# Down projection of an encoder kernel: loading rows into idle activation buffers, raising the corner splits' priority, and moving two late sums behind the first update of x

## The chip, the cores and the metric

The kernel runs on one core of one Trainium2 chip. The metric is device time in microseconds (us), the median of the runs shown; for the kernel before it is 1094.71 us.

The engines are named as the profile names them. PE is the matrix engine and PEld its weight load, DVE the vector engine, ACT the scalar engine, POOL the general engine, SP the engine that issues nearly all loads. A `q` behind a name is that engine's queue.

## The reference, cut to what matters

Two layers work on 256 tokens of 1024 numbers. Each layer is a gated feed-forward part of half weight, an attention part, and a second feed-forward part. The change touches the feed-forward part alone, and there the last product, the down projection by `w_down`:

```python
def swiglu(x, w_gate, w_up, w_down):
    return (jax.nn.silu(x @ w_gate) * (x @ w_up)) @ w_down

x = x + 0.5 * swiglu(rms_norm(x, ffn1_norm[l]), ffn1_w_gate[l], ffn1_w_up[l], ffn1_w_down[l])
```

`w_down` is 2816 x 1024, so a layer has two down projections and the program has four.

## The kernel before, in words

**Tiles.** The tokens lie in T = 2 tiles of 128 partitions. The 2816 inner columns are cut into NFC = 11 chunks of 256. For each chunk and token tile the gate and up columns are multiplied (24 matmuls of 512 columns in `project`), ACT makes the silu (`sg`), DVE the product (`hh`, line 435), and PE turns it round (`turn`). When all chunks have been started, `down` multiplies by `w_down`.

**Three products for one.** All large products are split: a value is written as a high part, rounded by ACT (line 181), and a low part, the rest, which DVE subtracts (line 182). `three` (lines 166 to 169) then issues three matmuls: high by high, low by high, high by low. The high and low parts of weights are `wh` and `wl`, in rings of 6 buffers; what comes from memory is `raw`, in a ring of RAW = 4 buffers of 512 KB. A new load into a `raw` buffer waits until the four-back user has been read by ACT and DVE.

**Seven products for eight.** A chunk c of the down projection takes two blocks of 128 rows of `w_down`, r0 = row block 2c and r1 = 2c + 1, each of two halves of 512 columns. `PLAN = "SFGFGFGSGSS"` says how each chunk is done. S is plain: 8 products of a 128 x 128 block by 512 columns (two rows, two token tiles, two halves). F and G do it with 7 products of sums and differences. Those need the corner (the first half of r0, split into `ch` and `cl`), the two halves of r1, and two tiles of differences: u holds r1 - r0 of the second halves and the difference of r0's halves, v holds r1's halves less parts of u. DVE makes u and v in four subtractions (line 343), and both are split like any weight. For F chunks (1, 3, 5) the differences are made and split earlier, during the gate and up products, and stored, so that `sevens` loads only half of r0 and all of r1 (256 and 512 KB). For G chunks (2, 4, 6, 8), the unprepared pairs, everything is done in place, and both rows are loaded whole. In all cases product "1", the corner, comes first. I write F1, G2, F3, G4, F5, G6, S7, G8, S9, S10 for the chunks by number.

**The corner has one pair of buffers.** `ch` and `cl` lie in the two buffers of tag `xg`; the next chunk's corner can be split only when PE has read the present one.

**The end.** The seven products gather in seven banks; after G8, `combine` adds the banks into x: lines 405 to 418 make the sums `p1`, `p16` and `ends` and add three of them, with the bank of product "1", to the four quarters of x. The last chunks S9 and S10 go on gathering in four banks, in `out_rows`, and for each quarter (t, d) line 299 adds half of the bank to x at high priority. Four products after a quarter's last one, `norm` starts on that quarter for the next stage: PE turns it round (line 198). In the fourth feed-forward part the quarters are stored instead.

**What orders the work.** PE's order is the order in which the code is written. On the other engines and on SP a scheduler sets it, by priorities and by its own forecast of time; each engine then works strictly in that order, so a waiting instruction holds all behind it.

**The idle buffers.** The normalized input of a feed-forward part is kept in four tiles, `xh0`, `xl0`, `xh1`, `xl1` (high and low part of the two token tiles), of 4 KB a partition each, as large as a `raw` buffer. PE reads them in `project` alone; after chunk 10's gate and up product of a token tile nothing reads that tile's pair until the next `norm` writes it.

Of the kernel before, what the change touches and what calls it, by code (L numbers as in the profile page):

```python
# [11 lines left out]
F32 = mybir.dt.float32  # L12
# [4 lines left out]
ALU = mybir.AluOpType  # L17
# [4 lines left out]
P = 128  # L22
# [4 lines left out]
T = S // P  # L27
KD = D // P
FC = 256
NFC = FF // FC  # L30
# [11 lines left out]
RAW = 4  # L42
# [13 lines left out]
def hybrid_encoder(ctx, tc, x, w_gu1, w_d1, w_in, b_gate, qk_gain, rpb, sink, t5,  # L56
# [123 lines left out]
    def split_to(hi, lo, src):  # L180
        linked("act", lambda: nc.scalar.activation(hi, src, AF.Copy))  # L181
        linked("dve", lambda: nc.vector.tensor_tensor(lo, src, hi.bitcast(F32), ALU.subtract))  # L182
# [99 lines left out]
        tag, n = ACC[t][d]  # L282
        return ps_acc.tile([P, 512], F32, name="acc", tag=tag, bufs=n)

    def out_rows(get, acc, k0, k1, last, w, l, scale, after):
        pieces = [(k, *rows(w, l, k)) for k in range(k0, k1)]
        for t in range(T):
            for d in range(2):
                for k, wh, wl in pieces:
                    first = acc[t][d] is None  # L290
                    if first:
                        acc[t][d] = out_bank(t, d)
                    xh, xl = get(t, k)
                    three(acc[t][d], xh, xl, wh[:, d, :], wl[:, d, :], first, last and k == k1 - 1)
                    tick(1)
                if last:
                    xd = xs[t][:, d * 512:(d + 1) * 512]
                    with tc.high_priority(500):
                        nc.vector.scalar_tensor_tensor(xd, acc[t][d], scale, xd, op0=ALU.mult, op1=ALU.add)
                    after(t, d)  # L300

    def ffn(l, n, w_gu, w_d, after):
        with tc.tile_pool(name="ffn", bufs=1) as fp:
# [30 lines left out]

            stored = {}

            def block_row(k, c0=0, n=2):
                r = ring.tile([P, 2, 512], F32, name="raw", tag="raw", bufs=RAW)[:, :n, :]
                nc.sync.dma_start(r, w_d[l, k * P:(k + 1) * P, :n * 512].rearrange("p (h n) -> p h n", h=n))
                return r  # L340

# [28 lines left out]

            def down():
                acc = [[None] * 2 for _ in range(T)]
                banks = {"2": (0, 0), "3": (0, 1), "4": (1, 0)}
                extra = {}
                c = 0
                while c < NFC:
                    if PLAN[c] == "S":
                        end = NFC if "S" * (NFC - c) == PLAN[c:] else c + 1
                        out_rows(get, acc, 2 * c, 2 * end, end == NFC, w_d, l, 0.5, after)
                        c = end  # L380
                        continue
                    final = c == max(PLAN.rindex("F"), PLAN.rindex("G"))
                    for name, slot, (wh, wl) in sevens(c):
                        if name in banks:
                            t, d = banks[name]
                            first = acc[t][d] is None
                            if first:
                                acc[t][d] = out_bank(t, d)
                            bank = acc[t][d]
                        else:  # L390
                            first = name not in extra
                            if first:
                                pool, tag = (ps_g, "g") if name in "16" else (ps_tp, "tp")
                                extra[name] = pool.tile([P, 512], F32, name=tag, tag=tag)
                            bank = extra[name]
                        three(bank, *[h[:, slot, :] for h in hs[c]], wh, wl, first, final and name in extra)
                        tick(1)
                    if final:
                        combine(extra)
                    c += 1  # L400

            def combine(acc):
# [4 lines left out]
                def plus(to, name, x):  # L407
                    nc.vector.scalar_tensor_tensor(to, acc[name], 0.5, x, op0=ALU.mult, op1=ALU.add)
                    return to

                u2 = plus(p1[:, 1, :], "6", p1[:, 0, :])
                u3 = plus(p16[:, 0, :], "7", u2)
                u4 = plus(p16[:, 1, :], "5", u2)
                u5 = plus(ends, "5", u3)
                plus(xs[0][:, :512], "1", xs[0][:, :512])
                for (t, d), u in (((0, 1), u4), ((1, 0), u3), ((1, 1), u5)):
                    xd = xs[t][:, d * 512:(d + 1) * 512]
                    nc.vector.tensor_tensor(xd, xd, u, ALU.add)

            for c in range(NFC):  # L420
                first = n == 0 and c == 0
# [391 lines left out]
```

## Time and profile before

| | |
|---|---|
| median of 3 runs | 1094.71 us (1093.98 to 1096.26) |
| profiled execution | 1094.91 us, of which the span is 1093.1 us |
| busy in the span: PE, PEld, DVE | 1079.0, 889.3, 855.3 us |
| busy: ACT, POOL | 659.2, 116.2 us |
| granted TensorE clock | 1.0 |
| loads | 211.60 MB through SP's queue, 61.5% of 16 engines' span |

The profile is of one execution. The page gives sums over the whole span; the timeline gives instructions in order of time with, in brackets, how long the engine was idle before and what ended it; the list of waits groups these idle times; the chain shows what was released by what, back from the last instruction. A matmul's duration overlaps the next one, so that its worth in time is the step from one start to the next. The first down projection's matmuls start at 135.4 us, and its next stage at about 194 us.

### The profile page before, as it was taken

What the parts mean: (1) busy time and instruction counts of PE and PEld (TensorE: products, weight loads), DVE (VectorE), ACT (ScalarE), POOL (GpSimd) and SP (SyncE); (2) the same over time, 40 slices, a digit from 0 to 9 for tenths busy, and PEclk for the clock granted to TensorE, in tenths of its full rate; (3) what the DMA queues carried; (4) which work ended last, traced back from release to release, by engine and by line L of the source; (5) the groups of instructions that cost most, each with busy time, mean ns of one, the idle gap of its engine ahead of it and who ended that gap; (6) DMA issues with size and microseconds to landing.
All of it is one profiled execution on the core that took longest, in us unless ns stands there. A gap on an engine that the chain in (4) does not pass through costs nothing.

```text
span 1093.1 us, 14659 instructions
## 1 busy us (share of the span) xinstructions
PE 1079.0 (99%) x5137; PEld 889.3 (81%) x5137; DVE 855.3 (78%) x1298; ACT 659.2 (60%) x1002; POOL 116.2 (11%) x118
## 2 busy tenths in 40 slices
PE   9999999999999999999999999999999999999998
PEld 7888878888888888887888888788888888888877
DVE  6887778889886778776877786787888767878676
ACT  6665544788764566554465665457877546656442
POOL 1400000243510000000000000003534000000000
PEclk9999999999999999999999999999999999999999
DMA  7876556765654666654757665557666555776553
GB/s 239 267 222 210 185 169 206 232 189 154 192 176 136 209 213 214 210 194 149 245 175 227 215 217 168 189 161 236 185 186 182 177 168 162 226 234 202 183 174 105
DMA packets 98827, 212.62 MB, mean 195 GB/s; under 512 B 7569, under 2 KB 13745, under 8 KB 98753
## 3 DMA queue, kind: packets, MB, share of 16 engines
q1 hardware_dynamic: 98560, 211.60, 61.5%
q8 instruction: 40, 0.66, 0.2%
q0 software_dynamic: 192, 0.08, 0.1%
q14 instruction: 35, 0.28, 0.1%
HBM read 210.59 MB, written 1.06 MB: 194 GB/s over the span
## 4 chain that ended last, share of the span: by engine, by line
PE 78%; DVE 10%; DMA 6%; issue 3%; ACT 3%; DVEq 0%; ACTq 0%
PE g L168 19%; PE g L169 19%; PE g L167 19%; DMA raw<-in_w_d 4%; DVE wl L182 4%; PE acc L167 4%; PE acc L168 4%; PE acc L169 4%; PE tp L314 2%; ACT wh L181 2%; PE tp L198 1%; DVE v L343 1%; PE g L234 1%; PE pt L557 1%; PE sc L536 1%
## 5 line engine op out<-in xcount | busy, mean ns | idle before, releaser
L182 DVE TENSOR_TENSOR wl<-raw,wh 128x1024 fp32r<-128x1024 f32 (+1 forms) x340 | 408.1, 1215 | 66.8 <-ACT wh L181 65.2
L181 ACT ACTIVATE wh<-raw 128x1024 fp32r<-128x1024 f32 (+1 forms) x340 | 349.8, 1045 | 158.6 <-DMA raw<-in_w_d 41.0
L167 PE MATMUL g<-wh,xh 128*128 128x512 f32 (+1 forms) x976 | 389.9, 399 | 0.0
L169 PE MATMUL g<-wh,xl 128*128 128x512 f32 (+1 forms) x976 | 379.0, 388 | 0.0
L168 PE MATMUL g<-wl,xh 128*128 128x512 f32 (+1 forms) x976 | 377.4, 387 | 0.4 <-DVE wl L182 0.4
L169 PEld LDWEIGHTS g<-wh,xl 128*128 128x128 f32 x976 | 183.3, 188 | 40.4 <-DVE xl L182 1.1
L168 PEld LDWEIGHTS g<-wl,xh 128*128 128x128 f32 x976 | 184.0, 189 | 32.1 <-DVE wl L182 0.8
L167 PEld LDWEIGHTS g<-wh,xh 128*128 128x128 f32 x976 | 183.5, 188 | 30.8 <-DVE hh L435 0.2
L433 ACT ACTIVATE sg<-g,rs_y 128x256 f32<-128x256 f32 x88 | 41.5, 471 | 135.3 <-PE g L169 133.8
L343 DVE TENSOR_TENSOR u<-raw 128x512 f32<-128x512 f32 x56 | 38.8, 693 | 79.5 <-DMA raw<-in_w_d 79.2
L167 PE MATMUL acc<-wh,hi 128*128 128x512 f32 x200 | 78.9, 395 | 0.0
L169 PE MATMUL acc<-wh,lo 128*128 128x512 f32 x200 | 78.0, 390 | 0.0
L168 PE MATMUL acc<-wl,hi 128*128 128x512 f32 x200 | 77.9, 389 | 0.0
L173 POOL TENSOR_TENSOR rs_y<-ms,mhalf 128x1 f32<-128x1 f32 x12 | 7.2, 602 | 659.5 <-DVE ms L219 652.5
L435 DVE SCALAR_TENSOR_TENSOR hh<-g,rs_y,sg 128x256 f32<-128x256 f32 x88 | 42.1, 479 | 38.2 <-ACT sg L433 38.0
L549 POOL TENSOR_TENSOR S<-S,sm 128x512 f32<-128x512 f32 x32 | 37.1, 1161 | 71.4 <-DVE sm L548 45.2
L169 PEld LDWEIGHTS acc<-wh,lo 128*128 128x128 f32 x200 | 37.5, 188 | 8.1
L168 PEld LDWEIGHTS acc<-wl,hi 128*128 128x128 f32 x200 | 37.6, 188 | 7.7
L167 PEld LDWEIGHTS acc<-wh,hi 128*128 128x128 f32 x200 | 37.6, 188 | 7.6
L542 ACT ACTIVATE S<-S,mx 128x256 f32<-128x256 f32 x64 | 31.8, 498 | 7.5 <-DVE mx L539 7.4
L314 PEld LDWEIGHTS tp<-ident,hh 128*128 128x128 f32 x176 | 24.5, 140 | 11.7 <-DVE hh L435 0.6
L314 PE MATMUL tp<-ident,hh 128*128 128x128 f32 x176 | 33.4, 272 | 0.0
(190 smaller groups left out, 1460.0 us busy)
## 6 DMA issues: line engine op xcount, KB each, us to landing
raw<-in_w_gu SPq DMA_DIRECT2D x176, 512.0 KB, 4.4
raw<-in_w_d SPq DMA_DIRECT2D x100, 512.0 KB, 4.4
raw<-in_w_in SPq DMA_DIRECT2D x64, 512.0 KB, 4.6
raw<-in_w_out SPq DMA_DIRECT2D x16, 512.0 KB, 3.5
bb<-in_b_gate SPq DMA_DIRECT2D x16, 256.0 KB, 3.7
raw<-in_w_bsw SPq DMA_DIRECT2D x8, 512.0 KB, 4.4
raw<-in_w_bna SPq DMA_DIRECT2D x8, 512.0 KB, 3.5
raw<-in_w_d SPq DMA_DIRECT2D x12, 256.0 KB, 3.6
```

Of the source, the lines that this page charges most:

```text
L167: nc.tensor.matmul(ps, xh, wh, start=first, stop=False)
L168: nc.tensor.matmul(ps, xh, wl, start=False, stop=False)
L169: nc.tensor.matmul(ps, xl, wh, start=False, stop=last)
L181: linked("act", lambda: nc.scalar.activation(hi, src, AF.Copy))
L182: linked("dve", lambda: nc.vector.tensor_tensor(lo, src, hi.bitcast(F32), ALU.subtract))
L198: nc.tensor.transpose(tp[:, i, :], xs[t][:, k * P:(k + 1) * P], ident)
L314: nc.tensor.transpose(tp[:, SLOT[t][i], :], hh[:, i * P:(i + 1) * P], ident)
L343: sub = lambda to, x, y: nc.vector.tensor_tensor(to, x, y, ALU.subtract)
L433: nc.scalar.activation(sg, ps[:, :FC], AF.Silu, scale=rstd[t])
L435: nc.vector.scalar_tensor_tensor(hh, ps[:, FC:], rstd[t], sg, op0=ALU.mult, op1=ALU.mult)
L542: nc.scalar.activation(S_[:, t, :], S_[:, t, :], AF.Exp, bias=mx[:, t:t + 1], scale=-1.0, accum_out=sm[:, t:t + 1])
L549: nc.gpsimd.tensor_tensor(S_, S_, sm.unsqueeze(2).to_broadcast([P, T, S]), ALU.mult)
```

## The change

Four things are changed, all in the down projection.

1. `block_row` takes a tag. The two rows of a G chunk go into the idle tiles: r0 into `xh0` or `xh1`, r1 into `xl0` or `xl1`, by turns over the G chunks (G2 and G6 use token tile 0's pair, G4 and G8 token tile 1's). F chunks stay in the `raw` ring. Loads into these tiles wait for PE's last reading of the normalized input, or for the last reader of the row that lay there before.
2. The corner's split gets priority 60.
3. `combine` first adds the bank of product "1" and the quarter (0, 1); `ends` and the two additions to the second token tile (`rest`) are issued behind the first line-299 update of x. `ends` becomes the tile itself that is added; no sum is dropped.
4. The unused argument `c0` goes away.

PE executes the same matmuls in the same order, and POOL's order is the same.

```diff
-    def out_rows(get, acc, k0, k1, last, w, l, scale, after):
+    def out_rows(get, acc, k0, k1, last, w, l, scale, after, rest=None):
...
-                        nc.vector.scalar_tensor_tensor(xd, acc[t][d], scale, xd, op0=ALU.mult, op1=ALU.add)
+                        updated = nc.vector.scalar_tensor_tensor(xd, acc[t][d], scale, xd, op0=ALU.mult, op1=ALU.add)
+                    if rest and t + d == 0:
+                        with tc.issue_after(updated.ins):
+                            rest()
...
-            def block_row(k, c0=0, n=2):
-                r = ring.tile([P, 2, 512], F32, name="raw", tag="raw", bufs=RAW)[:, :n, :]
+            def block_row(k, n=2, tag=None):
+                if tag:
+                    r = act.tile([P, 2, 512], F32, name="row", tag=tag)
+                else:
+                    r = ring.tile([P, 2, 512], F32, name="raw", tag="raw", bufs=RAW)[:, :n, :]
...
-                r0 = block_row(2 * c, n=1 if c in stored else 2)
-                r1 = block_row(2 * c + 1)
+                t = PLAN[:c].count("G") % T
+                r0 = block_row(2 * c, 1) if c in stored else block_row(2 * c, tag=f"xh{t}")
+                r1 = block_row(2 * c + 1, tag=None if c in stored else f"xl{t}")
                 corner = [act.tile([P, 512], F32R, name=f"c{p}", tag="xg", bufs=2) for p in "hl"]
-                split_to(*corner, r0[:, 0, :])
+                with tc.high_priority(60):
+                    split_to(*corner, r0[:, 0, :])
...
+                def add(t, d, u):
+                    xd = xs[t][:, d * 512:(d + 1) * 512]
+                    nc.vector.tensor_tensor(xd, xd, u, ALU.add)
+
+                plus(xs[0][:, :512], "1", xs[0][:, :512])
                 u2 = plus(p1[:, 1, :], "6", p1[:, 0, :])
                 u3 = plus(p16[:, 0, :], "7", u2)
                 u4 = plus(p16[:, 1, :], "5", u2)
-                u5 = plus(ends, "5", u3)
-                plus(xs[0][:, :512], "1", xs[0][:, :512])
-                for (t, d), u in (((0, 1), u4), ((1, 0), u3), ((1, 1), u5)):
-                    xd = xs[t][:, d * 512:(d + 1) * 512]
-                    nc.vector.tensor_tensor(xd, xd, u, ALU.add)
+                add(0, 1, u4)
+
+                def rest():
+                    plus(ends, "5", u3)
+                    add(1, 0, u3)
+                    add(1, 1, ends)
+
+                return rest
```

The change moves instructions at three places, which are the same in all four down projections; the numbers in the names are those of the first one. The rows of G2 are 1390 (r0) and 1392 (r1), of G4 1470 and 1472, of G6 1550 and 1552, of G8 1633 and 1635; the half rows of F3 and F5 are 1437 and 1517, their whole rows 1439 and 1519. Corner low parts are `cl_1395` (G2), `cl_1442` (F3), `cl_1475` (G4), `cl_1522` (F5), `cl_1555` (G6).

On SP, before, the loads of `w_down` from G2's first row on stood in the order of the chunks:

```order
L339 DMA raw_1390<-in_w_d1 128x1024
L339 DMA raw_1392<-in_w_d1 128x1024
L339 DMA raw_1437<-in_w_d1 128x512
L339 DMA raw_1439<-in_w_d1 128x1024
L339 DMA raw_1470<-in_w_d1 128x1024
L339 DMA raw_1472<-in_w_d1 128x1024
L339 DMA raw_1517<-in_w_d1 128x512
L339 DMA raw_1519<-in_w_d1 128x1024
L339 DMA raw_1550<-in_w_d1 128x1024
L339 DMA raw_1552<-in_w_d1 128x1024
```

On SP, after, from the same place:

```order
L345 DMA raw_1437<-in_w_d1 128x512
L345 DMA raw_1439<-in_w_d1 128x1024
L345 DMA raw_1517<-in_w_d1 128x512
L345 DMA row_1390<-in_w_d1 128x1024
L345 DMA row_1392<-in_w_d1 128x1024
L345 DMA raw_1519<-in_w_d1 128x1024
L345 DMA row_1470<-in_w_d1 128x1024
L345 DMA row_1472<-in_w_d1 128x1024
L345 DMA row_1552<-in_w_d1 128x1024
L139 DMA raw_1597<-in_w_d1 128x1024
L345 DMA row_1635<-in_w_d1 128x1024
L345 DMA row_1550<-in_w_d1 128x1024
```

The F rows moved ahead of G2's, and G6's r0 (`row_1550`) moved behind its own r1 and behind G8's r1, since its tile is G2's r0, whose last reader is G2's corner.

On DVE, before, around G4's differences:

```order
L182 TENSOR_TENSOR cl_1395<-raw_1390,ch_1394 128x512
L343 TENSOR_TENSOR u_1482<-raw_1472,raw_1470 128x512
L343 TENSOR_TENSOR v_1489<-raw_1472,u_1482 128x512
L182 TENSOR_TENSOR wl_1479<-raw_1472,wh_1478 128x1024
L343 TENSOR_TENSOR v_1489<-raw_1472,v_1489 128x512
L182 TENSOR_TENSOR wl_1486<-u_1482,wh_1485 128x1024
L182 TENSOR_TENSOR cl_1442<-raw_1437,ch_1441 128x512
L182 TENSOR_TENSOR wl_1493<-v_1489,wh_1492 128x1024
L182 TENSOR_TENSOR cl_1475<-raw_1470,ch_1474 128x512
```

On DVE, after, from G2's corner to G4's:

```order
L182 TENSOR_TENSOR cl_1395<-row_1390,ch_1394 128x512
L182 TENSOR_TENSOR wl_1486<-u_1482,wh_1485 128x1024
L182 TENSOR_TENSOR cl_1442<-raw_1437,ch_1441 128x512
L349 TENSOR_TENSOR u_1562<-row_1552,row_1550 128x512
L349 TENSOR_TENSOR u_1562<-row_1550 128x512
L182 TENSOR_TENSOR wl_1493<-v_1489,wh_1492 128x1024
L182 TENSOR_TENSOR wl_1526<-raw_1519,wh_1525 128x1024
L349 TENSOR_TENSOR v_1569<-row_1552,u_1562 128x512
L182 TENSOR_TENSOR wl_1559<-row_1552,wh_1558 128x1024
L182 TENSOR_TENSOR cl_1475<-row_1470,ch_1474 128x512
```

G4's differences now stand ahead of G2's corner, and G6's differences stand between F3's corner and G4's. In the same way G8's differences (`u_1645`, from 1633 and 1635) now stand between F5's corner and G6's.

On DVE at the end of the first down projection, as one piece of the difference; `x0_82<-acc_1319` is the line-299 update of the first quarter of x, the L408 and L416 rows are `plus`, the L418 and L421 rows are the additions:

```order
 L182 TENSOR_TENSOR wl_1836<-raw_1833,wh_1835 128x1024
-L408 SCALAR_TENSOR_TENSOR ends_1682<-tp_1375,p16_1681 128x512
-L418 TENSOR_TENSOR x1_83<-x1_83,p16_1681 128x512
 L299 SCALAR_TENSOR_TENSOR x0_82<-acc_1319,x0_82 128x512
-L418 TENSOR_TENSOR x0_82<-x0_82,p16_1681 128x512
-L418 TENSOR_TENSOR x1_83<-x1_83,ends_1682 128x512
+L416 SCALAR_TENSOR_TENSOR ends_1682<-tp_1375,p16_1681 128x512
+L421 TENSOR_TENSOR x1_83<-x1_83,p16_1681 128x512
+L421 TENSOR_TENSOR x0_82<-x0_82,p16_1681 128x512
+L421 TENSOR_TENSOR x1_83<-x1_83,ends_1682 128x512
```

The first update of x moved ahead of `ends` and of one addition.

More of the change, by code (lines that the diff above doesn't have):

```diff
@@ L373, in down @@
                 banks = {"2": (0, 0), "3": (0, 1), "4": (1, 0)}
-                extra = {}
+                extra, rest = {}, []
                 c = 0
@@ L378, in down @@
                         end = NFC if "S" * (NFC - c) == PLAN[c:] else c + 1
-                        out_rows(get, acc, 2 * c, 2 * end, end == NFC, w_d, l, 0.5, after)
+                        out_rows(get, acc, 2 * c, 2 * end, end == NFC, w_d, l, 0.5, after, *rest)
                         c = end
@@ L398, in down @@
                     if final:
-                        combine(extra)
+                        rest.append(combine(extra))
                     c += 1
```

## The prediction

> **What bounds the kernel now.** I read the page first.
>
> ```profile
> PE 1079.0 (99%) x5137; PEld 889.3 (81%) x5137; DVE 855.3 (78%) x1298; ACT 659.2 (60%) x1002; POOL 116.2 (11%) x118
> ```
>
> PE is busy for 1079.0 of 1093.1 us, and the change leaves its matmuls as they are. So only PE's waits can be won or lost. The list of waits, with those of PE and its weight load picked out, says which of them lie in the down projection (total us, times, longest).
>
> ```profile
> PEld g L168 <- DVE cl L182: 6.0, 8, 1.3
> ...
> PEld tp L198 <- DVE x L299: 2.5, 3, 0.8
> ```
>
> Eight times the weight load waits for a corner's low part, 6.0 us in all; three times the turning round of x waits for the update of x. The timeline of PE at 150 us shows what one such wait costs.
>
> ```profile
> 145.98 0.39 PE L167 MATMUL g<-ch,hi 128*128 128x512 f32 x1
> ...
> 150.74 0.39 PE L167 MATMUL g<-ch,hi 128*128 128x512 f32 x1
> ...
> 151.37 0.19 PEld L168 LDWEIGHTS g<-cl,hi 128*128 128x128 f32 x1 [0.67 <-DVE cl L182]
> ...
> 151.71 0.40 PE L169 MATMUL g<-ch,lo 128*128 128x512 f32 x1
> ...
> 186.27 0.39 PE L169 MATMUL acc<-wh,lo 128*128 128x512 f32 x1
> 187.08 0.66 PE L198 MATMUL tp<-ident,x 128*128 128x128 f32 x4 [0.42 <-DVE x L299]
> ...
> 190.36 0.60 PE L198 MATMUL tp<-ident,x 128*128 128x128 f32 x4
> ```
>
> The corner matmuls of G2 and F3 start 4.76 us apart; that is 21 matmuls of 0.227 us. F3's third matmul, due 0.45 after its first at 151.19, starts at 151.71: the weight load's 0.67 costs PE 0.52. Taking 0.15 off each of the eight, 6.0 us of waiting is 6.0 - 8 x 0.15 = **4.8 us** of time, at F3 and F5 of each of the four down projections, 1.2 us a projection. At the end, 187.08 - 186.27 - 0.227 = 0.58 us, three times: **1.75 us**.
>
> The timeline of DVE shows why F3 waits.
>
> ```profile
> 146.55 0.69 DVE L343 TENSOR_TENSOR u<-raw 128x512 f32<-128x512 f32 x1 [2.48 <-DMA raw<-in_w_d]
> 147.16 0.69 DVE L343 TENSOR_TENSOR v<-raw,u 128x512 f32<-128x512 f32 x1
> 147.76 1.22 DVE L182 TENSOR_TENSOR wl<-raw,wh 128x1024 fp32r<-128x1024 f32 x1
> 148.90 0.69 DVE L343 TENSOR_TENSOR v<-raw,v 128x512 f32<-128x512 f32 x1
> 149.50 1.22 DVE L182 TENSOR_TENSOR wl<-u,wh 128x1024 fp32r<-128x1024 f32 x1
> 150.63 0.68 DVE L182 TENSOR_TENSOR cl<-raw,ch 128x512 fp32r<-128x512 f32 x1
> ```
>
> G4's second row lands late, DVE stands 2.48 us, and F3's corner is queued behind five steps of G4. Steps follow each other every 0.60 us (512 columns) or 1.14 us (1024 columns). The corner ends at 151.31, 0.40 before the third matmul; so a corner costs nothing if it ends no later than 0.05 after its chunk's first matmul was due.
>
> **What goes.** Loads, from the chain of waits (start, time to landing):
>
> ```profile
> 127.08 5.01 DMA raw<-in_w_d
> ...
> 136.91 4.04 DMA raw<-in_w_d
> ...
> 142.90 3.63 DMA raw<-in_w_d
> ...
> 153.30 4.42 DMA raw<-in_w_d
> ...
> 498.96 3.59 DMA raw<-in_w_d
> ```
>
> 3.6 us is a load with little beside it, 4 to 5 one with others in flight. G4's second row, sent at 142.90 before, can now go when PE has finished the second token tile's last gate product, which two rows of ACT date (it waits for PE before each).
>
> ```profile
> 129.74 0.48 ACT L433 ACTIVATE sg<-g,rs_y 128x256 f32<-128x256 f32 x1 [3.75 <-PE g L169]
> ...
> 131.34 1.06 ACT L181 ACTIVATE wh<-raw 128x1024 fp32r<-128x1024 f32 x1 [0.64 <-PE g L169]
> ...
> 135.50 0.48 ACT L433 ACTIVATE sg<-g,rs_y 128x256 f32<-128x256 f32 x1 [0.32 <-PE g L169]
> ```
>
> The first token tile's last product is done at 129.7, the second's at 135.5. So that row leaves at about 135.6 and lands near 140.5, six us earlier. F3's and F5's corners then stand behind nothing that is late: F3's is the second step after G2's corner, 1.14 + 0.68 later, near 148, with 2.8 us to spare. All 4.8 us go from these two places.
>
> The end: in the old order DVE reached the update of x thus.
>
> ```profile
> 184.01 1.21 DVE L182 TENSOR_TENSOR wl<-raw,wh 128x1024 fp32r<-128x1024 f32 x1
> 185.15 0.68 DVE L408 SCALAR_TENSOR_TENSOR ends<-tp,p 128x512 f32<-128x512 f32 x1
> 185.75 0.68 DVE L418 TENSOR_TENSOR x<-x,p 128x512 f32<-128x512 f32 x1
> 186.34 0.68 DVE L299 SCALAR_TENSOR_TENSOR x<-acc,x 128x512 f32<-128x512 f32 x1
> ...
> 187.54 0.68 DVE L418 TENSOR_TENSOR x<-x,ends 128x512 f32<-128x512 f32 x1
> ```
>
> Two steps of 0.60 fall behind it, it ends at 185.83, and PE, due at 186.50, no longer waits: all 1.75 us go. Behind it stand `ends`, three additions and a normalization step, so that the second quarter's update starts six steps of 0.60 after 185.15 and ends at 189.4; PE, 0.58 earlier than in the row of 190.36, needs it at 189.8. ACT's squares wait for the last addition, which stays at 187.55. I put this reordering at nothing; if the 0.4 us of cover is gone, it costs up to 0.4 us three times.
>
> **What comes.** Now G2, G4 and G6. Corners are due at 145.98 + 0.05 = 146.03, and every two chunks (9.52 us) later: 155.55 and 165.07.
>
> *G2.* Its second row left at 127.08 before; now both rows wait for PE to finish the first token tile's last product (129.7), and on SP the F rows moved ahead of them. Row 1392 leaves near 129.9 with three or four loads in flight; at a time between 4.04 and 5.01, I take 4.6, it lands at 134.5. From there DVE has, these steps up to G2's corner: eight of 0.60 (u and v of G2 and G4, one of the hidden values), five of 1.14, one `hh`, and the corner, 0.68 to its end.
>
> ```profile
> 137.93 0.48 DVE L435 SCALAR_TENSOR_TENSOR hh<-g,rs_y,sg 128x256 f32<-128x256 f32 x1
> 138.33 1.21 DVE L182 TENSOR_TENSOR wl<-v,wh 128x1024 fp32r<-128x1024 f32 x1
> ```
>
> With 0.40 for `hh` that is 4.8 + 5.7 + 0.4 + 0.68 = 11.58. The corner ends at 146.1: on the edge, 0.05 late. It is 145.7 at the earliest, since DVE first splits F1's row, whose high part ACT starts at 131.34: 1.06, 1.14 and 0.60 later the second step of u can start, at 134.15. It is 146.7 if the load takes 5.2, a little over the 5.01.
>
> *G4.* `row_1550` lies in the tile of `row_1390`, so its load waits on SP for G2's corner, and DVE waits at `u_1562`, the step after F3's corner, for that load. Behind it in DVE's queue are `wl_1493`, `wl_1526`, G6's v, and G4's own corner. The load follows `row_1635` by about 1 us; I take 4.42. Then u twice, wl three times, v and the corner: 3 x 0.60 + 3 x 1.14 + 0.68 = 5.90. The corner ends at 146.1 + 4.42 + 5.90 = 156.4: 0.85 late.
>
> *G6.* In the same way `row_1633` waits for G4's corner and DVE for it; nothing else was sent just before, so 3.63. Then four steps of 0.60, three of 1.14 and the corner, 6.50: 156.4 + 3.63 + 6.50 = 166.55, due 165.07: **1.5 us** late in all (G4's 0.85 and 0.65 more). ACT's halves of these splits end earlier by these sums and add nothing; G8's corner has S7's 5.4 us before it.
>
> With both loads at 3.59 and G2 at 145.7 the lateness is 0.2 a projection; with both at 4.42 and G2 at 146.7 it is 2.9. I take 1.5, since the rows nearest in kind (one behind another load, one alone) are 4.42 and 3.63. Four projections: 6.0 us.
>
> The Trainium skill, in "DMA: Bandwidth & Descriptors" (section "Anatomy of one DMA — SWDGE (gpsimd) path"), fits a transfer as about 2.0 us plus its bytes at 436 GB/s; as an estimate by that page 512 KB takes 3.2 us, and the same sum gives corners at 155.2 and 164.9, on time, a total near 1088. That is another queue's fit; these loads take 3.59 and more here.
>
> Elsewhere: PE's and POOL's orders are the same, DVE's and ACT's in the attention part too. On SP two bias loads go ahead of a weight load there, which ACT took up after waiting for PE and not for the load:
>
> ```profile
> 202.92 0.63 ACT L181 ACTIVATE wh<-raw 128x512 fp32r<-128x512 f32 x1 [0.73 <-PE g L169]
> ```
>
> I put that at nothing, at worst 0.5 us. The `xh` and `xl` tiles are read last by G8's corner, some 20 us before `norm` writes them.
>
> **Sum.** On the profiled execution, 1094.91 us: -4.8 - 1.75 + 6.0 = -0.55, so 1094.36. The median shown is 0.20 lower: **1094.2 us**, no change that can be told, since about 0.2% (2.2 us) is what a measurement of this kernel can tell.
>
> **Rivals.** *All corners come in time.* With loads of 3.59 and G2's corner at 145.7, 0.2 us a projection stays: 0.8 - 6.55 = -5.75, 1089.0; half as much lateness as I took (0.75) gives -3.55, 1091.2. It is faster by over 2.2 us once lateness is under 1.1 a projection. For it: the row of 3.59, and that SP sends G4's second row seven us earlier. Against it: 4.42 and 5.01 where loads meet, and DVE's queue, which holds G4's corner behind a load that cannot leave before G2's. The Trainium skill's "Perfetto Trace Analysis" (section "Optimization Strategy") reads a gap that repeats as a possible lack of buffers; by that rule more buffers should close it. Chance 0.28.
>
> *The chain through the tiles is longer than two chunks of PE.* Corner, load, differences, next corner is one loop; PE gives it 9.52 us. At 4.42 for both loads and G2's row landing at 135.1, lateness is 2.9: 11.6 - 6.55 = +5.05, 1099.8. It decides from a lateness of 2.2 a projection, 0.7 more than I sum. For it: G2's row now leaves 2.8 us later than before, behind more loads. Chance 0.22.
>
> *The first update doesn't come sooner*, because the scheduled order rests on a sum that DVE reaches later than before: 1.75 us stay, 1095.9, still no change. It is the weaker part of my own 0.50, with 0.08 of it.
>
> **How the numbers follow.** No change 0.50 (1094.2), faster 0.28, slower 0.22. The range runs from 1091.0, half the lateness, to 1098.0, a lateness of 2.4 a projection; what lies beyond is under 2 in 10. Within no change alone it is 1092.5 to 1096.9.
>
> **What would show it.** In the profile after: the wait of PEld for `cl` still there, some 7 us over about eight times, but at 155 and 166 us, not at 151 and one F chunk (9.5 us) later; DVE's `u` waiting for `row` just before them, by about 2 us each; the wait of L198 for L299 gone; F3's and F5's corners without a gap. I am wrong if G4 and G6 show no gap, if F3 or F5 keeps one, or if G2's corner is late by more than 0.7 us.

## The result and the profile after

The changed kernel takes 1104.43 us (median of six runs, 1101.41 to 1108.57), the one before 1094.32 us beside it. The ratio is 1.0089, with an interval of 1.0066 to 1.0111: slower by 10 us, and above the range of the prediction. The profiled execution took 1104.77 us with a span of 1103.0, 9.9 us more than before.

The list of waits of the changed kernel, with the rows of PE, its weight load and DVE that answer to those shown of before (total us, times, longest):

```profile
DVE u L349 <- DMA row<-in_w_d: 21.9, 17, 3.6
...
PEld tp L167 <- DVE lo L182: 7.8, 4, 2.3
PEld g L168 <- DVE cl L182: 7.4, 7, 2.1
```

The wait for `cl` is still there, as forecast at other places than before; the wait of L198 for L299 (2.5 us) is gone. A new row stands above both: four times, once in each down projection, PE waits for a `lo` that DVE splits. That row belongs to no term of the prediction. The timeline of PE in the first projection shows the place, and what follows it:

```profile
145.69 0.39 PE L169 MATMUL acc<-vh,lo 128*128 128x512 f32 x1
147.91 0.50 PE L167 MATMUL tp<-uh,hi 128*128 128x512 f32 x1 [1.84 <-DVE lo L182]
148.25 0.39 PE L168 MATMUL tp<-ul,hi 128*128 128x512 f32 x1
...
149.38 0.63 PE L169 MATMUL g<-ch,lo 128*128 128x512 f32 x1
...
151.94 0.58 PE L169 MATMUL acc<-wh,lo 128*128 128x512 f32 x1
152.36 0.39 PE L167 MATMUL tp<-wh,hi 128*128 128x512 f32 x1
```

It is F1's product "7". It gathers in a bank of the pool `tp`, and this bank holds the turned hidden values of chunk 10 until DVE has split them. It was due at 145.69 + 0.227 = 145.92 and starts at 147.91: 2.0 us late. Before, it started in step, 0.23 us behind the product ahead of it (145.07):

```profile
145.30 0.39 PE L167 MATMUL tp<-uh,hi 128*128 128x512 f32 x1
```

In the changed kernel eight matmuls behind it start 0.43 us apart in place of 0.227 (from 148.95, the start ahead of 149.38, to 152.36), 1.6 us more. The table by stretches gives the granted clock, the last but two of its columns:

```profile
149.40:152.40 3.00, 3.00 (x9) 2.36 (x8) 0.89 (x2) 0.63 (x1) 0.00 (x0) 0.51 0.91 314
152.40:155.00 2.60, 2.60 (x13) 2.16 (x12) 1.72 (x3) 1.41 (x2) 0.00 (x0) 1.00 0.54 203
```

DVE's timeline shows why that `lo` is late:

```profile
135.58 0.69 DVE L349 TENSOR_TENSOR u<-row 128x512 f32<-128x512 f32 x1 [1.75 <-DMA row<-in_w_d]
136.89 0.69 DVE L349 TENSOR_TENSOR u<-row 128x512 f32<-128x512 f32 x1 [0.61 <-DMA row<-in_w_d]
...
142.50 1.28 DVE L349 TENSOR_TENSOR u<-row 128x512 f32<-128x512 f32 x2
143.71 0.68 DVE L349 TENSOR_TENSOR v<-row,u 128x512 f32<-128x512 f32 x1
144.31 1.22 DVE L182 TENSOR_TENSOR wl<-raw,wh 128x1024 fp32r<-128x1024 f32 x1
145.44 0.68 DVE L349 TENSOR_TENSOR v<-row,v 128x512 f32<-128x512 f32 x1
146.04 1.22 DVE L182 TENSOR_TENSOR wl<-row,wh 128x1024 fp32r<-128x1024 f32 x1
147.18 0.68 DVE L182 TENSOR_TENSOR lo<-tp,hi 128x512 fp32r<-128x512 f32 x1
147.78 0.68 DVE L182 TENSOR_TENSOR cl<-row,ch 128x512 fp32r<-128x512 f32 x1
```

Before, the same stretch read so:

```profile
141.04 0.69 DVE L343 TENSOR_TENSOR u<-raw 128x512 f32<-128x512 f32 x1 [1.50 <-DMA raw<-in_w_d]
141.65 1.22 DVE L182 TENSOR_TENSOR wl<-raw,wh 128x1024 fp32r<-128x1024 f32 x1
142.79 0.68 DVE L182 TENSOR_TENSOR lo<-tp,hi 128x512 fp32r<-128x512 f32 x1
143.39 0.68 DVE L182 TENSOR_TENSOR cl<-raw,ch 128x512 fp32r<-128x512 f32 x1
```

One subtraction of G4 stood ahead of that `lo` then; now all four and a split of G4's row do, and DVE itself comes to all this 2.4 us later than I reckoned, because G2's second row landed just before the second `u`, at 136.9, and not at 134.5. That row was issued 0.38 us behind its pair's first one, at 130.03, and took 6.8 us. What the loads into the idle tiles took in this window is in the last line of the view by tile:

```profile
DMA to landing us min/median/max: 3.5/5.9/6.8
```

The other three projections come to the same stall in part by another row. There G2's second row took 5.2, 5.7 and 4.5 us; in the second and the fourth, DVE waits again at G4's own rows, of which the second took 6.5 and 6.6 us, and `lo` stands behind that too. The fourth projection on DVE, where `lo` then starts at 1051.07:

```profile
1045.77 0.69 DVE L349 TENSOR_TENSOR u<-row 128x512 f32<-128x512 f32 x1 [0.84 <-DMA row<-in_w_d]
1046.99 0.69 DVE L349 TENSOR_TENSOR u<-row 128x512 f32<-128x512 f32 x1 [0.52 <-DMA row<-in_w_d]
```

One corner wait, the longest, is G4's in the second projection (PE, then DVE):

```profile
516.28 0.39 PE L167 MATMUL g<-ch,hi 128*128 128x512 f32 x1
518.30 0.50 PE L168 MATMUL g<-cl,hi 128*128 128x512 f32 x1 [1.63 <-DVE cl L182]
```
```profile
512.34 1.29 DVE L349 TENSOR_TENSOR u<-row 128x512 f32<-128x512 f32 x2 [3.60 <-DMA row<-in_w_d]
...
517.56 0.68 DVE L182 TENSOR_TENSOR cl<-row,ch 128x512 fp32r<-128x512 f32 x1
```

This is the loop as foretold: G6's differences wait for a load that could not leave before G2's corner, and G4's corner stands behind them.

Where the 9.9 us came from, each from distances between PE's starts, less 0.227, with 0.11 for the first step behind a wait (147.91 to 148.25):

| | us |
|---|---|
| F1's "7" waits for `lo`: 2.00, 1.61, 1.38, 1.72, and 4 x 0.11 | +7.2 |
| half clock behind the first of them | +1.6 |
| corners of G4 and G6, seven waits: 5.6, and 7 x 0.11 | +6.3 |
| `xl` at the start of the third feed-forward part | +0.8 |
| `hh` at 141.5 | +0.4 |
| corners of F3 and F5: 3.8, and 8 x 0.11 | -4.7 |
| L198 for L299, three times | -1.75 |
| sum | +9.85 |

### The profile page after: what moved, and what is told of

It is laid out like the page before. It is cut to its first block, busy times and chain, and to the rows that moved or that the text cites. A ratio compares the mean times of both kernels' runs of the same rounds, so it can differ in the third digit from the quotient of the medians.

```text
span 1103.0 us, 14661 instructions
## 1 busy us (share of the span) xinstructions
PE 1081.4 (98%) x5137; PEld 889.9 (81%) x5137; DVE 856.1 (78%) x1298; ACT 657.7 (60%) x1002; POOL 115.3 (10%) x118
## 5 line engine op out<-in xcount | busy, mean ns | idle before, releaser
L182 DVE TENSOR_TENSOR wl<-raw,wh 128x1024 fp32r<-128x1024 f32 (+1 forms) x324 | 388.7, 1214 | 76.7 <-ACT wh L181 75.2
L181 ACT ACTIVATE wh<-raw 128x1024 fp32r<-128x1024 f32 (+1 forms) x324 | 332.0, 1043 | 122.1 <-PE g L169 36.4
L167 PE MATMUL g<-wh,xh 128*128 128x512 f32 (+1 forms) x976 | 389.8, 399 | 0.0
L167 PEld LDWEIGHTS g<-wh,xh 128*128 128x128 f32 x976 | 183.6, 188 | 30.7 <-DVE hh L451 0.2
L167 PE MATMUL acc<-wh,hi 128*128 128x512 f32 x200 | 79.5, 397 | 0.0
L349 DVE TENSOR_TENSOR u<-raw 128x512 f32<-128x512 f32 x24 | 16.6, 691 | 40.2 <-DMA raw<-in_w_d 40.1
L167 PEld LDWEIGHTS acc<-wh,hi 128*128 128x128 f32 x200 | 37.8, 189 | 7.7
L349 DVE TENSOR_TENSOR u<-row 128x512 f32<-128x512 f32 x32 | 21.2, 688 | 23.0 <-DMA row<-in_w_d 21.9
```

Of the source, the lines that this page charges most:

```text
L167: nc.tensor.matmul(ps, xh, wh, start=first, stop=False)
L349: sub = lambda to, x, y: nc.vector.tensor_tensor(to, x, y, ALU.subtract)
```

## The experiments

**Theory A:** the loss lies in DVE's order. Steps that wait for late loads (G4's and G6's subtractions) stand ahead of steps that PE needs sooner (the split of the last hidden values, the corners). **Theory B:** the loads into the idle tiles land too late, and the order on DVE is secondary. The first two runs take one part of the change alone.

### The late sums alone

The kernel before with the diff's edits of `out_rows` and `combine`: `rest` behind the first update of x, nothing else.

> The kernel before with only the late sums tied behind x's first update; the rows stay in the raw ring. Theory A (the loss comes from the order on DVE that the new rows bring, the late sums are a small gain): PE's wait at L198 for L299 goes, three times 0.58 us, everything else stays: about 1.75 us less than before, ratio 0.998 to 0.999, and the waits for cl at F3 and F5 (6.0 us) are still there. Theory B (the loss comes from the rows' own loads) says the same here. A third view, that the tie itself brings part of the loss, would give a time above the one before.

Measured: 1094.78 us, ratio 0.9997 (0.9988 to 1.0006). The wait of L198 for L299 is gone, as all said, but little or nothing is gained. DVE's timeline and then PE's say why:

```profile
552.60 3.48 DVE L182 TENSOR_TENSOR wl<-raw,wh 128x1024 fp32r<-128x1024 f32 x3
556.00 0.68 DVE L205 TENSOR_TENSOR xg<-tp,x 128x512 f32<-128x512 f32 x1
556.60 0.68 DVE L182 TENSOR_TENSOR xl<-xg,xh 128x512 fp32r<-128x512 f32 x1
```
```profile
557.34 0.50 PE L169 MATMUL g<-wh,xl 128*128 128x512 f32 x1 [0.65 <-DVE xl L182]
```

With the tie the schedule puts three splits of weights together, ahead of the `xg` and `xl` that the third feed-forward part needs first; before, there were two (553.49, 2.35 us, and `xl` at 555.76). PE waits 0.81 us there, in every kernel with the tie below but one. The rest of the 1.75 us went in this profile to single waits that come and go between runs (an `hh` at 394 us, 0.54, and a `pt` at 840, 0.22 longer than before); the corners cost 6.0 us in the list, as before. So the size isn't settled by this run; that the tie moves `xl` is.

### The rows alone

The kernel before with these lines only (and the tag of `block_row`):

```diff
+                t = PLAN[:c].count("G") % T
+                r0 = block_row(2 * c, 1) if c in stored else block_row(2 * c, tag=f"xh{t}")
+                r1 = block_row(2 * c + 1, tag=None if c in stored else f"xl{t}")
```

> The kernel before with only the rows in the idle tiles; no tie of the late sums. Theories A and B both: all the loss is here, 1.75 us more than in the changed kernel's profile, so about 1104 to 1107, ratio about 1.010; DVE's low split of the last turned hidden values is again ended near 147.9, and PE's first tp product waits 1.5 to 2 us for it in each of the four down projections. If the time is under 1100, tie and rows disturb each other, and neither theory is complete.

Measured: 1106.45 us, ratio 1.01 (1.0083 to 1.0117). All the loss is in the rows: `PEld tp L167 <- DVE lo L182` is 8.5 us over four times, 2.0 us of PE at each of the first three and 1.5 at the last; behind two of those of 2.0 us the clock was halved for about eight matmuls.

The corners' raised priority does nothing that the traces show. This run lacks it as well as the tie, and on every engine its order of instructions differs from the changed kernel's at the same places, and in the same way, as the order of the kernel before differs from that of the tie alone. The priority by itself was not run.

### The low split of the hidden values first

```diff
+                gate = turned[NFC - 1] if c == 4 else None
-                us, vs = stored.get(c) or differences(r0, r1, lambda name, r: parts(r))
+                us, vs = stored.get(c) or differences(r0, r1, lambda name, r: parts(r), gate)
```

(`differences` issues its four subtractions behind `gate` on DVE; `turned` keeps the split of the turned hidden values. The rest is the changed kernel.)

> The changed kernel with one bond more: G4's four subtractions stand behind chunk 10's low split of the hidden values (lo from tp) on DVE. The loads and SP's order stay as they are. Theory A: that split ends before 146, PE's wait for it (6.7 us over four projections, and 1.6 us at half clock behind the first) goes, and the lateness of G4's and G6's corners stays or grows by 0.6: 1104.8 - 6.7 - 1.6 gives about 1096 to 1098. Theory B (late landing of G2's pair): PE's waits only move from the hidden values to G2's corner, and the time stays within 2 us of the changed kernel's, 1102 to 1105.

Measured: 1096.79 us, ratio 1.0017 (1.0007 to 1.0026). The wait for `lo` is gone and the clock is 1.0; 7.6 us less than the changed kernel, inside what A expected and far from B. G2's second row took 4.6, 5.7, 6.3 and 6.7 us in the four projections of this profile, so the wait for `lo` goes with late rows too. The corners' wait stays in all:

```profile
PEld g L168 <- DVE cl L182: 7.3, 9, 1.5
```

But it isn't where A had it. G4's corner is nearly in time. G2's, still behind two of G4's subtractions, keeps PE waiting 0.2 to 0.5 us in each projection, and G6's 0.6 to 1.2 us.

### Each G chunk's subtractions behind the corner ahead of them

```diff
-                with tc.high_priority(60):
-                    split_to(*corner, r0[:, 0, :])
+                cut[c] = split_to(*corner, r0[:, 0, :])
+                gate = cut.get(c - 1) or cut.get(c - 2)
```

(This is against the changed kernel; `differences` takes `gate` as above.)

> The changed kernel with each G chunk's four subtractions bonded behind the corner split of the chunk ahead of it on DVE (G4's behind F3's, and so behind the last hidden values' low split too), without the raised priority. Theory A: a corner no longer stands behind subtractions that wait for a load, and a load into a reused tile leaves sooner; the waits for lo (6.7 us and 1.6 us of half clock) and most of the later corner waits (5.9 us) go: 1104.8 - 8.3 - 5 gives about 1088 to 1093. Theory B (the loads land too late whatever DVE's order): G4's and G6's differences come too late instead, PE then waits at their third or fifth product, and the time stays over 1097.

Measured: 1093.29 us, ratio 0.9984 (0.9975 to 0.9993), some 11 us under the changed kernel, with the same loads in the same tiles. DVE:

```profile
136.03 0.69 DVE L355 TENSOR_TENSOR u<-row 128x512 f32<-128x512 f32 x1 [1.99 <-DMA row<-in_w_d]
137.28 0.69 DVE L355 TENSOR_TENSOR u<-row 128x512 f32<-128x512 f32 x1 [0.56 <-DMA row<-in_w_d]
...
145.16 0.68 DVE L182 TENSOR_TENSOR lo<-tp,hi 128x512 fp32r<-128x512 f32 x1
145.76 0.68 DVE L182 TENSOR_TENSOR cl<-row,ch 128x512 fp32r<-128x512 f32 x1
148.30 0.69 DVE L182 TENSOR_TENSOR cl<-raw,ch 128x512 fp32r<-128x512 f32 x1 [1.86 <-ACT ch L181]
148.91 1.29 DVE L355 TENSOR_TENSOR u<-row 128x512 f32<-128x512 f32 x2
```

The first pair lands 0.4 us later still than in the changed kernel, and `lo` comes two us sooner and in time. So it isn't the landing by itself: a late row costs PE nothing at F1 when `lo` doesn't stand behind what waits for it. What stays is 0.2 to 0.3 us at G4's and G6's corners, since F3's corner has to wait for PE (1.86 us idle) and all of G4 waits behind it.

### The bond one corner further back

```diff
-                gate = cut.get(c - 1) or cut.get(c - 2)
+                gate = cut.get(c - 2) if c > 3 else None
```

> Like the run with each G chunk's subtractions behind the corner ahead of it, but the bond goes to the corner of the G chunk two back, so that u and v run in the 1.9 us in which DVE waits for F3's corner. That run kept a wait of 0.2 to 0.3 us of PE at the corners of G4 and G6, 2.0 us in all, because eight steps stood between F3's corner and G4's. Theory A (only DVE's order was wrong, the idle tiles are good): these 2.0 us go too, 1093.3 - 2.0 = about 1091.3, ratio to before 0.996 to 0.998. Theory B (the loads into the idle tiles land too late): u waits for its load ahead of F3's corner now, and F3 waits again as before; 1093 to 1096.

Measured: 1090.9 us, ratio 0.9966 (0.9955 to 0.9978). No wait of PE or PEld for `cl` or for the hidden values' `lo` is left. A load into a reused tile still waits for a corner here; with the corners in time that loop costs nothing.

### The same order, and no row in an idle tile

The tie and the bond behind the corner ahead stay; all rows go into the ring:

```diff
-                r0 = block_row(2 * c, 1) if c in stored else block_row(2 * c, tag=f"xh{t}")
-                r1 = block_row(2 * c + 1, tag=None if c in stored else f"xl{t}")
+                r0 = block_row(2 * c, 1 if c in stored else 2)
+                r1 = block_row(2 * c + 1)
```

> The rows stay in the raw ring as before; the late sums are tied, and each G chunk's subtractions stand behind the corner split ahead of them on DVE. No row in an idle tile. Theory A, strict form (DVE's order is all that counts, the place of the rows nothing): F3's and F5's corners no longer stand behind a late load, and the time is that of the same order with the idle tiles, 1091 to 1094. Rival (the idle tiles are needed, since a row in the ring leaves only when a buffer comes free): F3 to G6 wait elsewhere, for wl of the second row or for a difference, and the time is 1095 or more.

Measured: 1089.68 us, ratio 0.996 (0.9947 to 0.9972), not to be told from the run above. DVE:

```profile
143.09 0.68 DVE L182 TENSOR_TENSOR lo<-tp,hi 128x512 fp32r<-128x512 f32 x1
...
147.88 1.22 DVE L182 TENSOR_TENSOR wl<-raw,wh 128x1024 fp32r<-128x1024 f32 x1 [3.50 <-ACT wh L181]
149.02 0.68 DVE L182 TENSOR_TENSOR cl<-raw,ch 128x512 fp32r<-128x512 f32 x1
```

G4's second row is as late as before the change, but only one step that waits for it, the split at 147.88, stands ahead of F3's corner (149.02), and not five. What the change was to gain at F3 and F5 is had by order alone.

### Longer stalls

The order with the bond two back; the low split of chunk 10 alone is repeated, and G2's corner stands behind the repeats:

```diff
+EXTRA = {0: 4, 2: 5, 3: 6, 5: 7}
...
+                        for _ in range(EXTRA[n]):
+                            turned[c] = linked("dve", lambda: nc.vector.tensor_tensor(lo, tp, hi.bitcast(F32), ALU.subtract))
```

> The order with the bond to the corner two back (about 1091 to 1093), with chunk 10's low split of the hidden values repeated 4, 5, 6 and 7 times more in the four projections (0.60 us each, same values), all ahead of G2's corner. PE's product that needs that PSUM bank was due 0.41, 0.74, 0.69 and 0.45 us after the split's end, so it should now wait about 2.0, 2.3, 2.9 and 3.75 us, 10.9 in all. Theory A (PE waits for the bank): all of that is seen at that product, and the time is 1102 to 1104 if the clock stays. If a stall of 2 us or more halves the clock behind it as after the first stall of the changed kernel (eight matmuls 0.427 us apart in place of 0.227, 1.6 us), three or four such stretches give 1107 to 1110. Theory B: PE has other work to fill it or waits elsewhere anyway; under 1096.

Measured: 1111.05 us, ratio 1.0152 (1.0138 to 1.0166). The repeats in the first projection on DVE, the product on PE, and the clock behind the four stalls (by stretches):

```profile
145.98 2.87 DVE L336 TENSOR_TENSOR lo<-tp,hi 128x512 fp32r<-128x512 f32 x4
```
```profile
145.58 0.39 PE L170 MATMUL acc<-vh,lo 128*128 128x512 f32 x1
148.99 0.47 PE L168 MATMUL tp<-uh,hi 128*128 128x512 f32 x1 [3.02 <-DVE lo L336]
```
```profile
149.00:153.00 4.00, 4.00 (x11) 3.14 (x12) 3.93 (x6) 1.58 (x2) 0.00 (x0) 0.57 0.48 131
509.30:512.30 3.00, 3.00 (x13) 2.50 (x14) 2.96 (x6) 1.56 (x2) 0.00 (x0) 1.00 0.40 126
697.00:702.50 5.50, 5.50 (x14) 4.30 (x15) 4.57 (x7) 1.75 (x3) 0.00 (x0) 0.50 0.58 174
1059.00:1064.50 5.50, 5.41 (x13) 4.31 (x14) 4.68 (x7) 1.58 (x2) 0.00 (x0) 0.52 0.45 112
```

PE waits 3.19, 3.27, 3.86 and 4.76 us at that product, 15.1 in all. That is longer than I set: a repeat took 0.72 us (2.87 / 4) and not 0.60, and the split itself came later in this run. But what is put on the split is seen in full at the product, so PE does wait for that bank. Three of the four stalls are followed by half the clock, the one of 3.27 us isn't.

### The first pair in the ring

```diff
+                idle = c not in stored and c > 2
+                r0 = block_row(2 * c, tag=f"xh{t}") if idle else block_row(2 * c, 1 if c in stored else 2)
+                r1 = block_row(2 * c + 1, tag=f"xl{t}" if idle else None)
```

> The changed kernel, except that G2's two rows stay in the raw ring, so that they leave before 127.1 as in the kernel before; G4, G6 and G8 use the idle tiles, and DVE's order at chunk 10's low split is as in the changed kernel, behind G4's subtractions. Theory A: G2's rows are no longer late, but G4's subtractions still wait for its second row, near 141.7; five steps later the low split ends at 146.5, 0.6 us after the product was due; 0.6 to 1.3 us of waiting stays in each projection, and the time is 1097 to 1101. Theory B (the late landing of G2's pair is the cause): the stall for the hidden values goes altogether, and the time is under 1096.

Measured: 1094.83 us, ratio 0.9999 (0.9988 to 1.0011). B's number, but not B's picture; DVE and PE:

```profile
141.37 0.69 DVE L349 TENSOR_TENSOR u<-row 128x512 f32<-128x512 f32 x1 [0.54 <-DMA row<-in_w_d]
...
145.45 0.68 DVE L182 TENSOR_TENSOR lo<-tp,hi 128x512 fp32r<-128x512 f32 x1
```
```profile
146.19 0.50 PE L167 MATMUL tp<-uh,hi 128*128 128x512 f32 x1 [0.74 <-DVE lo L182]
```

The stall for `lo` stays, 0.90, 1.09, 0.45 and 1.08 us, about what A gave. I had not seen that this edit also frees G6: token tile 0's pair now goes to G6, whose rows leave near 129.5 and are there long before they are used, and G4's and G6's corners wait 0.4 us in all. So the edit takes away two delays at once and can't tell them apart.

### The later rows in the ring

G2 and G4 in the idle tiles, G6 and G8 in the ring; against the run above:

```diff
-                idle = c not in stored and c > 2
+                idle = c not in stored and c < 5
```

> The counterpart of the run with the first pair in the ring: the changed kernel, with G2's and G4's rows in the idle tiles and those of G6 and G8 in the raw ring, so that no load waits for a corner split any more, while G2's pair is as late as in the changed kernel and chunk 10's low split stands behind G4's subtractions as there. If the loop corner, load into the reused tile, differences, next corner makes the waits at G4's and G6's corners: these (5.6 us in the changed kernel) go and the waits for the hidden values (6.7 us and the half clock) stay: 1104.4 - 5.6 = about 1099. Rival (G2's late pair alone makes DVE late through to G6): the waits at G4 and G6 stay too and the time is 1102 or more.

Measured: 1104.37 us, ratio 1.0082 (1.0064 to 1.01). The corners' wait is 5.7 us over six times: the rival's number. But the loop was not cut, it went through the ring. DVE:

```profile
150.60 0.68 DVE L182 TENSOR_TENSOR cl<-raw,ch 128x512 fp32r<-128x512 f32 x1
...
154.89 0.69 DVE L349 TENSOR_TENSOR u<-raw 128x512 f32<-128x512 f32 x1 [1.14 <-DMA raw<-in_w_d]
```

G6's second row left at 151.31, when F3's corner (150.60, and 0.68) gave a buffer of the ring free, and G4's corner stood behind it as before. How the 6.3 us at the corners divide between the late first pair and the loop stays open; what these two runs and the one with the bond two back show is that each of the two does harm only through what stands behind the waiting subtractions.

### Two checks on the tie

The kernel with all rows in the ring and the right order, first with the kernel before's `combine`:

> Like the run with the rows in the raw ring and each G chunk's subtractions behind the corner ahead of them, but without the tie of the late sums: the wait of L198 for L299 comes back (0.58 us, three times) and the wait for xl near 555 us (0.83 us) goes, because two splits of weights stand ahead of that xl on DVE in place of three. Theory A (the tie nets 1.75 - 0.83 = 0.9 us, since it moves that xl): 1089.7 + 0.9 = about 1090.6. Rival (the tie is worth the full 1.75 us, and the wait for xl comes from something else): 1091.4 and the wait for xl stays. Second rival (the tie is worth nothing): 1089.7.

Measured: 1090.31 us, ratio 0.9963 (0.995 to 0.9977). The wait for `xl` is gone and that for L299 is back, as A said; the times of the three cases lie within their uncertainty.

Then with the tie in all projections but the second:

```diff
-                        rest.append(combine(extra))
+                        tail = combine(extra)
+                        rest.append(tail) if n != 2 else tail()
```

> Like the run with the rows in the raw ring, the corner order and the tie, but the second down projection, the one that a feed-forward stage follows, isn't tied. Theory A: the wait for xl near 555 us (0.83) goes, the wait of L198 for L299 comes back there only (0.58): 0.25 us less, about 1089.4, and nothing else moves. Rival (xl waits for another reason): the wait stays and the time is 1090.3.

Measured: 1089.31 us, ratio 0.9954 (0.9941 to 0.9968). The wait for `xl` at 555 us is gone, and L198 waits 0.67 us at 540.65 only. By its median it is the fastest kernel of the study, though its spread overlaps that of the others with the right order; it is ahead of both kernels compared here, and it has no row in an idle tile.

### The later rows idle, in the right order

The kernel with the first pair in the ring, and the bond of the run two back:

```diff
+                gate = cut.get(c - 2) if c > 3 else None
```

> G2's rows in the raw ring, those of G4, G6 and G8 in the idle tiles, the late sums tied, and the subtractions bonded behind the corner two chunks back. It asks whether the idle tiles are worth anything once DVE's order is right. Theory A (they are worth nothing: in the ring the rows come in time for the right order): as with all rows in the ring, 1089 to 1091. Rival (the idle tiles gain when only the first pair stays out of them): under 1089, with the waits for hh or for the first x of a stage gone as well.

Measured: 1090.45 us, ratio 0.9959 (0.9946 to 0.9973), as with all rows in the ring. With the right order the idle tiles bring nothing that can be told.

## Why the prediction was wrong

*F3 and F5, -4.8.* Right: their waits are gone, and 4.7 us with them. *The end, -1.75.* Right for L198. Wrong in what I put "at nothing": the reordering costs 0.81 us at another place, the `xl` of the third feed-forward part, a stage later than I looked; the bound was 0.4 us three times at the second quarter.

*G4 and G6, +6.0.* Right in place and kind. That the sum agrees (6.3 measured) is luck. From the end of G2's corner to the end of G4's the rows give 10.8 to 11.8 us, where I had 10.32, and from G4's to G6's 10.1 to 10.4, where I had 10.13; so the loop lost more per turn than I summed. But PE, held up at F1, came later to these corners itself and saw less of it: 0.3, 2.7, 1.7 and 1.6 us in the four projections, where I had 1.5 in each.

*The step that failed* is G2's term, "on the edge, 0.05 late", which put G2's price at next to nothing. PE lost 7.2 us there, at F1's product "7", and 1.6 more at half clock, for which I had no term. The term had two faults.

The larger one is the time of the loads. For G2's second row "I take 4.6", up to 5.2; it took 6.8, 5.2, 5.7 and 4.5 us in the four projections. G4's second row was to land "near 140.5", 4.9 us after it left; it took 6.5 and 6.6 in the second and the fourth, where DVE waited for it. The list of steps behind the landing was right: from there to the end of G2's corner I had 11.58 us, and the rows give 136.89 to 147.78 + 0.68, 11.57. So with the landing measured in the first projection my own sum would have put G2's corner 2.4 us late there. My own mark, G2's corner late by more than 0.7 us, is passed: it ends at 148.46, 2.4 late.

The other fault is in reading that list: "u and v of G2 and G4, one of the hidden values". I counted that hidden value's split as 0.60 us in DVE's queue and took the corner for the first thing that PE needs from this chain. But PE needs the split itself, for its bank, three matmuls ahead of the corner. With G2's corner ended at 146.1, as I had it, the split would have ended 0.6 earlier, at 145.5, against a product due three matmuls ahead of the corner's 145.98, at 145.30: some 0.25 us a projection, 1 us in all, would by this estimate have been the price of the oversight by itself.

What I took as given, and the runs showed to be the lever, is the order: rows as late as these cost PE nothing at F1 once `lo` and the corner stand ahead of G4's subtractions (1093.29 and 1090.9).

*The load.* My values came from rows of loads that left 0.6 us or more apart. Here two of 512 KB left 0.38 us apart behind two others. The estimate by the Trainium skill's "DMA: Bandwidth & Descriptors" (section "Anatomy of one DMA — SWDGE (gpsimd) path"), 3.2 us, is about half of the median of 5.9 us above.

*The rivals.* "The chain through the tiles is longer than two chunks of PE" has the right sign, and a reason that holds ("G2's row now leaves 2.8 us later, behind more loads"), but its price of +5.05 is not what happened: PE lost at G4's and G6's corners what I summed, and the rest came at F1. "All corners in time" is what the right order gives: 1090.9 with the rows in the idle tiles. The Trainium skill's "Perfetto Trace Analysis" (section "Optimization Strategy"), quoted there, reads a gap that repeats as a possible lack of buffers. Here more buffers did close the gap at F3 and F5 (4.7 us), but they opened others, and an order of steps closed it with no buffer more (1089.68).

*What stays open:* why the runs of the changed kernel spread over 7 us (those of before over 2.3). The profiles show first pairs that took 4.1 and 5.2 us in one kernel and 6.1 and 7.0 in another, which would do it, and within the changed kernel's profile G2's second row took 4.5 to 6.8 us; but no run varied that alone.

## What to carry to other kernels

When loads are moved, follow the strict queue of the engine that consumes them: list every step behind the first one that can wait, and for each ask which engine needs it, for its data and for the bank or buffer that it gives back. A step that waits for memory belongs behind those that have their data and that the bounding engine needs next; that order was worth about 4 us here with no buffer more (1094.70 to 1090.31 without the tie), and a head start for loads without it cost 10. A tie of a few sums can move a wait into the next stage, so look one stage past the edit.

## What the runs showed of the hardware

*A stall of 2 us can halve PE's clock.* Of ten stalls at F1's product of 1.99 to 4.76 us (changed kernel 1, rows alone 3, longer stalls 4, later rows in the ring 2), seven were followed by a granted clock of about 0.5, with matmuls 0.43 us apart for 7 to 13 of them, 1.4 to 2.7 us of loss each; 3.27 us and two of 2.00 us were not. Of those up to 1.8 us none was. The Trainium skill's "TensorE: Matmul & The Clock Gate" (section "Part 1: The HAM clock gate (the "warmup" mystery)") gives half clock after an idle window of about 3.4 us, counted by a free-running window. The spacing of 0.427 us agrees with it, and so does the grid of 3.413 us told next; that 2.0 us are enough does not.

*Which stall is followed by half the clock is a matter of where it falls.* Each of these seven halvings lasts 3.41 us (148.92 to 152.33 in the changed kernel) or twice that, and those of one run begin whole multiples of 3.413 us apart: in the run with longer stalls at 149.53, 695.66 and 1057.47, which is 160 and 106 times 3.413. So the clock here changes on a grid of 3.413 us. In the piece of the grid ahead of each of the seven, PE is busy for 1.58 us or less by the profile (1.57 from 145.51 to 148.92 in the changed kernel). The three stalls that weren't followed by one are cut by the grid in such a way that in no piece PE is busy for less than 1.68 us: the stall of 3.27 us leaves 1.68 and 2.03. PE needn't be idle for a whole piece, and a longer stall that the grid cuts can cost less than a shorter one that it doesn't. This is read from ten stalls; no run set the limit on purpose, and at the end of the program it is less sharp (in the changed kernel's last piece with matmuls PE is busy for 1.5 us, and the clock falls one piece later).

*A step on DVE that needs the one just before it starts later.* The same subtraction five times over the same tile ran every 0.72 us, against 0.60 for steps that don't need each other. The two steps of v in the run with all rows in the ring, of which the second reads the first's result, are 0.72 us apart too (150.95 and 151.67).
